# Retention step of an encoder layer: inner products of four chunks ahead of the cross products, and the turns of the norm factor at another place and in another kind of bank

## Chip, core and metric

The kernel runs on one core of one Trainium2 chip. The metric is the device time of one execution in microseconds. Before the change it is 1183.5 us, the median of three runs (1183.13 to 1184.19).

## What is computed

One layer of a bidirectional encoder on 1024 tokens of width 1024, in float32: an input projection, eight heads of retention and eight heads of windowed attention beside each other, an output projection with a layer norm, and a gated feed-forward block with a second layer norm. The change touches only the retention, of which the reference says, for one direction and chunks of 128 tokens:

```python
scores = jnp.einsum('bhncd,bhnsd->bhncs', q, k) * decay_in[None, :, None]
y_inner = jnp.einsum('bhncs,bhnse->bhnce', scores, v)
kv = jnp.einsum('bhnsd,bhnse->bhnde', k * k_decay[None, :, None, :, None], v)
...
_, r_prev = lax.scan(step, jnp.zeros((b, h, d, d), q.dtype), jnp.moveaxis(kv, 2, 0))
...
y_cross = jnp.einsum('bhncd,bhnde->bhnce', q * q_decay[None, :, None, :, None], r_prev)
return (y_inner + y_cross).reshape(b, h, s, d)
```

Both directions are added, each head is normed over its 64 values (the mean is taken out of the values beforehand, so only a mean square is left), multiplied with a gain, and gated.

## The kernel before

**Stages.** The first 120 us or so hold the first projections and the attention of the first pair of heads. Then four rounds of retention follow, one for each pair of retention heads (up to about 358 us in the profile); rounds 1, 2 and 3 carry the attention of their pair beside it. After that come the output projection, the first norm, and the feed-forward block.

**The order on TensorE is written out by hand.** `run(steps, total)` takes a list in which `F` stands for a share of the remaining projection work: a queue of triples of 512-column matmuls (lines 77, 78, 79; `F` takes some three or four triples at a time). So the list says after which piece of projection each piece of retention or attention stands. The other engines' order is not written out: a scheduler places their instructions, so an edit of the list also changes the order on VectorE and ScalarE.

**Names in the list.** With `hh` or `q` 0 or 1 for the first and second half of the tokens (four chunks of 128 each):

- `K(q)`: keys turned on TensorE (line 404) and scaled by their decay on VectorE. `r.kv`: the state updates (line 423). `r.scan`: the recurrence over chunks on VectorE, and four DMAs that put the states in place. `Q(q)`: scores (line 454), decayed on VectorE into `pt`, and queries with decay `qq` (line 459).
- `Y(hh)`, `Retention.out`: for each of four chunks the inner products (`pt` with the values `rv`, line 475) and the cross products (`qq` with `states`, line 477), all four chunks in one PSUM bank of the kind "o"; then a square of it on ScalarE (line 480) and a copy into `y` on VectorE (line 481).
- `M(hh)`, `Retention.norm`: sums of the squares by a small matmul (line 488), a power on GpSimd (line 491), and the factor spread out to `r` on ScalarE (line 493).
- `X(hh)`, `Retention.turn`: four turns (transposes) of `r` on TensorE (line 498) into a bank of the kind "t", and one multiply `y * gain * turned factor` on VectorE (line 500), which reads that bank.
- `sco(n)`, `trn(n)`, `val(n)`: for block n of the attention, scores (lines 527, 528, softmax on VectorE and ScalarE in lines 529 to 539), turns of the probabilities (line 551, one bank of kind "t" for each of two key groups, each copied out by ScalarE into `ptr`, line 553), and values (line 563, `ptr` with `av`, in a bank of kind "o").
- `presplit_*`: side work on VectorE, ScalarE and the SP queue's DMAs (lines 580 to 582) for later weights; `G` are the decays of the next round.

**Banks.** Each kind of bank ("mm", "s", "t", "o") has two, taken in turn. A new user of a kind waits until the readers of the one before last are done. `X(1)` and `M(1)` of a round stand in the next round's list (as `X1` and `M1`).

In rounds 1 to 3 the part of the list that matters is, before:

```python
run([*V, K(0), M1, F, K(1), sco(0), F, (r.kv,), Q(0), F, sco(1), X1, F, trn(0), sco(2), (r.scan,), F, trn(1),
...
     G[2], X(0), Y(1), val(4), val(5), F, trn(6), F, trn(7), F], 48)
```

Of the kernel before, what the change touches and what calls it, by code (L numbers as in the profile page):

```python
# [16 lines left out]
P = 128  # L17
# [25 lines left out]
def layer(tc, xT, xn, w_first, w_mt, w_rv, w_out, w_pg, w_pe, pT, w_gu, w_dn,  # L43
          consts, dec_b, dec_c, sink, gng, lnp, out):
    nc = tc.nc
    act, dve, pool, pe, sp = nc.scalar, nc.vector, nc.gpsimd, nc.tensor, nc.sync
# [12 lines left out]
    def nm(s):  # L59
        uid[0] += 1  # L60
        return f"{s}{uid[0]}"

    def bank(tag, shape=(P, HF)):
        tag = ROLE[tag]
        return ps.tile(list(shape), F32, tag=tag, bufs=NB[tag], name=nm("b" + tag))
# [67 lines left out]
    def bt(shape, tag, bufs=None, dt=F32):  # L133
        return bpool.tile(list(shape), dt, tag=tag, bufs=bufs, name=nm(tag))
# [15 lines left out]
    with tc.manual_schedule(engines={mybir.EngineType.DVE, mybir.EngineType.SP}):  # L150
        for kt in range(KT):
            r = xraw[kt]
# [107 lines left out]
    for h in range(2):  # L260
        sl = slice(h * HF, (h + 1) * HF)
        b = st[1, h]
        for g in range(2):
            a = slice(64 * g, 64 * g + 64)
# [14 lines left out]
    def take(k):  # L279
        for _ in range(min(k, len(queue))):  # L280
            queue.pop(0)()
            ticks[0] += 1
            for what in (later, side):
                for x in [x for x in what if x[0] <= ticks[0]]:
                    what.remove(x)
                    x[1]()

    def mtile(idx, evac):
        hold = {}

        def load():
            hold["w"] = unit2(w_mt[idx])

        def step(h, kt):
            if kt == 0:
                hold["b"] = bank("mm")
            b, w = hold["b"], hold["w"][kt // 4]
            c = slice((kt % 4) * P, (kt % 4 + 1) * P)
            sl = slice(h * HF, (h + 1) * HF)
            mm3(b, w[:, 0, c], w[:, 1, c], xs[kt][:, 0, sl], xs[kt][:, 1, sl], kt == 0, kt == KT - 1)  # L300
            if kt == KT - 1:
                evac(b, h)

        return [load], [lambda h=h, kt=kt: step(h, kt) for h in range(2) for kt in range(KT)]

    def enqueue(tiles):

        def both(f, g):
            f()
            g()  # L310

        for f in tiles[0][0]:
            f()
        for n, (_, steps) in enumerate(tiles):
            if n + 1 < len(tiles):
                for k, f in enumerate(tiles[n + 1][0]):
                    steps[2 * k] = lambda f=f, g=steps[2 * k]: both(f, g)
            queue.extend(steps)
# [16 lines left out]
    rv = bt([P, NT, HF], "rv")  # L335
# [52 lines left out]
    class Retention:  # L388
# [76 lines left out]
        def out(self, hh):  # L465

            o, pt, qq = bank("o", (P, 4, P)), self.pt[hh], self.qq[hh]
            for j in range(4):
                n = 4 * hh + j
                for part in range(2):  # L470
                    for h in range(2):
                        a = slice(64 * h, 64 * h + 64)
                        v = self.i * P + 64 * h
                        if part == 0:
                            pe.matmul(o[a, j, :], rv[:, n, v:v + 64], pt[:, h, j, :], start=True, stop=False)
                        else:
                            pe.matmul(o[a, j, :], self.states[:, h, n, :], qq[:, h, j, :], start=False, stop=True)
            of = o.rearrange("p n c -> p (n c)")
            sq = self.sq = bt([P, HF], "rb")
            act.activation(sq, of, AF.Square)  # L480
            dve.tensor_copy(self.half(hh), of)
            self.o = o

        def norm(self, hh):

# [7 lines left out]
            act.activation(r.rearrange("p n h e -> p (n h) e"), sm[:, 1, :].unsqueeze(2).to_broadcast([P, 8, 64]), AF.Copy)  # L493

        def turn(self, hh):
            tb = bank("t", (P, 4, P))
            for j in range(4):
                pe.transpose(tb[:, j, :], self.r[hh][:, j].rearrange("p h e -> p (h e)"), ident)
            y = self.half(hh)
            dve.scalar_tensor_tensor(y, y, gn[:, self.i:self.i + 1], tb.rearrange("p n c -> p (n c)"), ALU.mult, ALU.mult)  # L500
# [167 lines left out]
    def ytile(k):  # L668
        if ys[k] is None:
            ys[k] = a_tile([P, S], "y", "A0" if k < 4 else "A1")  # L670
        return ys[k]
# [24 lines left out]
    def gate(i):  # L696
        def f(b, h):
            s = bt([P, HF], "sq", 1)
            sl = slice(h * HF, (h + 1) * HF)
            act.activation(s, b, AF.Tanh, scale=0.5)  # L700
            dve.scalar_tensor_tensor(s, s, 1.0, b, ALU.add, ALU.mult)
            dve.scalar_tensor_tensor(ys[2 * i][:, sl], s, 0.5, ys[2 * i][:, sl], ALU.mult, ALU.mult)
        return mtile(10 + i, f)

    def run(steps, total):

        shares = steps.count(None)
        done = n = 0
        for f in steps:
            if f is None:  # L710
                n += 1
                take(total * n // shares - done)
                done = total * n // shares
            else:
                f[0](*f[1:])

    F = None
    with tc.manual_schedule(engines={mybir.EngineType.PE}):
        enqueue([mtile(0, ev_av), proj_rv(), *project(1), *project(2), *project(3), gate(0), gate(1), gate(2), gate(3)])

        spare.append(bt([P, S], "aq", 3, F32R))
        twin = lambda t: t.rearrange("p (a b) -> p a b", a=2)
        ops = [twin(spare[1]), a_tile([P, 2, HF], "pro", "A0", F32R)]
        side.extend(presplit_out(0, ops, 17.5, 4))
        side.extend(presplit_out(1, ops, 44, 4, spare[:1]))
        a = Attention(0, ytile(1))
        sco, trn, val = (lambda n: (a.scores, n)), (lambda n: (a.turn, n)), (lambda n: (a.values, n))
        run([F, F, sco(0), F, sco(1), F], 16)
        run([F, (av_turn, 0), (av_turn, 1), F, trn(0), sco(2), F, trn(1), sco(3), F, val(0), val(1), trn(2), sco(4), F,
             trn(3), sco(5), F, val(2), val(3), trn(4), sco(6), F, trn(5), sco(7), F, val(4), val(5), trn(6), (decay_q, 0),  # L730
             F, trn(7), (decay_k, 0, 0), F, val(6), val(7), (decay_k, 0, 1), F], 64)
        assert not side and not later
        y0 = ytile(0)
        side.extend(presplit_gate())
        states = state_tile()
        r = Retention(0, y0, states)
        K, M = (lambda q: (r.keys, q)), (lambda q: (r.norm, q))
        Q, X = (lambda q: (r.scores, q)), (lambda q: (r.turn, q))
        Y = lambda hh: (r.out, hh)
        run([K(0), F, K(1), F, F, (r.kv,), Q(0), F, (r.scan,), F, F, F, Y(0), Q(1),  # L740
             F, M(0), (decay_q, 1), F, (decay_k, 1, 0), X(0), Y(1), (decay_k, 1, 1), F, F], 48)
        V = []
        for i in range(1, NPAIR):
            assert i == 1 or not side, len(side)
            M1, X1 = M(1), X(1)
            r = Retention(i, ytile(2 * i), states)
            a = Attention(i, ytile(2 * i + 1))
            if i == 2:
                late = [ytile(6), ytile(7)]
                op = twin(late[1].bitcast(F32R))  # L750
                side.extend(presplit_out(2, [op], 2, 3.5, late[:1]))
                side.extend(presplit_small(0, op, 30) + presplit_small(1, op, 38))
            elif i == 3:
                op = twin(bt([P, S], "aq", 3, F32R))
                side.extend(presplit_out(3, [op], 4, 3.5, [bt([P, S], "rk", 2)]))
                side.extend(presplit_small(2, op, 32) + presplit_small(3, op, 40))
            G = [(f, i + 1, *x) for f, x in ((decay_q, ()), (decay_k, (0,)), (decay_k, (1,)))] if i + 1 < NPAIR else \
                [(lambda: None,)] * 3
            run([*V, K(0), M1, F, K(1), sco(0), F, (r.kv,), Q(0), F, sco(1), X1, F, trn(0), sco(2), (r.scan,), F, trn(1),
                 sco(3), F, val(0), val(1), F, trn(2), sco(4), F, trn(3), sco(5), F,  # L760
                 Y(0), val(2), val(3), Q(1), F, G[0], trn(4), sco(6), M(0), F, G[1], trn(5), sco(7), F,
                 G[2], X(0), Y(1), val(4), val(5), F, trn(6), F, trn(7), F], 48)
            V = [val(6), val(7)]
        run([*V, M(1), F, X(1), F, F], 16)

# [179 lines left out]
    X = four("a")  # L945
    product(1, X, True, a11)
    part = ct([P, 8, HF], "h0b")
# [21 lines left out]
    X = four("a")  # L969
# [121 lines left out]
    X = four("a")  # L1091
# [4 lines left out]
    pt = {t: load_p(t) for t in range(2)}  # L1096
# [20 lines left out]
    for k in range(4):  # L1117
        c = slice(k * P, (k + 1) * P)
# [15 lines left out]
    pt = {t: load_p(t) for t in range(2)}  # L1134
    Y = four("a")
    product(6, Y, True, TT[2], steps[6:8])
    es3.close()
# [160 lines left out]
    n = 0  # L1298
    for k, upto in enumerate((2, 4, 8, 12)):
        c = slice(k * P, (k + 1) * P)  # L1300
# [311 lines left out]
    with tc.manual_schedule(engines={ET.PE, ET.DVE, ET.Activation, ET.Pool, ET.SP}):  # L1612
        ahead(2, 4)
        for k in range(NG):
# [5 lines left out]
            j = k + 1 - NG  # L1620
# [103 lines left out]
```

## Time and profile before

| what | value |
| --- | --- |
| median of three runs | 1183.5 us |
| the profiled execution's own time | 1184.56 us |
| its span (first to last instruction) | 1182.8 us |
| TensorE matmul busy | 1169.2 us (99%) |
| VectorE, ScalarE, GpSimd busy | 765.8, 534.5, 366.1 us |
| matmul busy from 288 to 358 us (round 3) | 68.66 of 70.00 us |
| matmul busy from 358 to 420 us (output projection) | 61.73 of 62.00 us |
| clock granted to TensorE | 0.998 of full speed |

Lines such as L498 are line numbers of the kernel before. A timeline row has the start, the duration, the engine, the line, the operation, what it writes and reads, and in brackets how long the engine was idle before it and what ended that. PE is the matmul side of TensorE, PEld its weight load, DVE is VectorE, ACT ScalarE, POOL GpSimd. Matmuls are pipelined and their ends are modelled, so the spacing of their starts says more than their durations; in a steady run of projection triples the starts stand 0.23 us apart.

### The profile page before, as it was taken

How to read it: one execution, taken by the hardware profiler on the slowest of the kernel's cores; microseconds unless marked ns; L12 is line 12 of the kernel's file. 1: busy time of each engine (PE TensorE's matmuls, PEld its weight loads, DVE VectorE, ACT ScalarE, POOL GpSimd, SP SyncE). 2: the span in 40 equal slices, each digit the busy share in tenths (PEclk: the TensorE clock that was granted, in tenths of full speed). 3: DMA queues.
4: the chain of work that ended last, by engine and by line, in shares of the span. 5: the costliest groups of instructions: out<-in, count | busy, mean ns of one | idle time of the engine just before them, and what ended most of it. 6: DMA issues, size and time to landing. Idle time of an engine off the chain costs nothing.

```text
span 1182.8 us, 17057 instructions
## 1 busy us (share of the span) xinstructions
PE 1169.2 (99%) x6068; PEld 969.6 (82%) x6068; DVE 765.8 (65%) x1310; ACT 534.5 (45%) x1049; POOL 366.1 (31%) x346
## 2 busy tenths in 40 slices
PE   9999999999999999999999999999999999999997
PEld 7888888888888888888888888888888888888885
DVE  4666678775759688948655455545545465774677
ACT  5566347776756266214333333323333325562463
POOL 2001020202010021004755657464655341134232
PEclk9999999999999999999999999999999999999999
DMA  6345656546345945756223322233113179999977
GB/s 252 101 149 215 241 184 234 192 141 214 105 161 213 373 169 192 280 183 209 109 81 131 134 90 86 91 134 134 66 68 134 72 214 320 348 276 200 268 179 213
DMA packets 80661, 211.71 MB, mean 179 GB/s; under 512 B 9536, under 2 KB 14784, under 8 KB 80576
## 3 DMA queue, kind: packets, MB, share of 16 engines
q1 hardware_dynamic: 71936, 193.84, 46.4%
q0 software_dynamic: 8640, 16.78, 8.1%
q8 instruction: 48, 0.79, 0.3%
q14 instruction: 37, 0.30, 0.1%
HBM read 139.29 MB, written 62.13 MB: 170 GB/s over the span
## 4 chain that ended last, share of the span: by engine, by line
PE 87%; ACT 5%; DVE 4%; DMA 2%; issue 1%; POOL 0%; DVEq 0%; SPq 0%; ACTq 0%; POOLq 0%
PE bs L783 6%; PE bs L781 6%; PE bs L782 6%; PE bt L781 6%; PE bt L783 6%; PE bt L782 6%; PE bmm L783 5%; PE bmm L781 5%; PE bmm L782 5%; PE bo L782 5%; PE bo L783 5%; PE bo L781 5%; PE bmm L77 4%; PE bmm L78 4%; PE bmm L79 4%; ACT sc L533 1%
## 5 line engine op out<-in xcount | busy, mean ns | idle before, releaser
L77 PE MATMUL bmm<-H,w 128*128 128x512 f32 x240 | 97.6, 407 | 0.0
L78 PE MATMUL bmm<-H,w 128*128 128x512 f32 x240 | 94.2, 392 | 0.0
L79 PE MATMUL bmm<-H,w 128*128 128x512 f32 x240 | 94.1, 392 | 0.0
L1185 POOL TENSOR_TENSOR H<-ln 128x512 f32<-128x512 f32 x22 | 28.9, 1313 | 179.3 <-DMA ln<-in_w_gu 179.3
L1215 POOL TENSOR_TENSOR ev<-ev 128x512 f32<-128x512 f32 x33 | 55.0, 1667 | 90.2 <-DVE ev L1230 39.1
L72 DVE TENSOR_TENSOR w<-H,w 128x512 fp32r<-128x512 f32 x44 | 41.3, 939 | 62.5 <-ACT w L71 62.5
L72 DVE TENSOR_TENSOR w<-raw,w 128x512 fp32r<-128x512 f32 x56 | 46.0, 827 | 50.4 <-ACT w L71 50.2
L524 POOL COPY sc<-skb 128x1 f32<-128x1 f32 x64 | 14.7, 238 | 186.2 <-PE bt L551 166.8
L1213 ACT ACTIVATE ev<-ev 128x512 f32<-128x512 f32 x33 | 20.9, 632 | 102.7 <-DVE ev L1230 102.7
L1219 POOL TENSOR_TENSOR ev<-ev,ev 128x512 f32<-128x512 f32 x44 | 62.7, 1437 | 2.6
L72 DVE TENSOR_TENSOR u<-H,u 128x512 fp32r<-128x512 f32 x47 | 38.1, 810 | 36.9 <-ACT u L71 36.6
L77 PEld LDWEIGHTS bmm<-H,w 128*128 128x128 f32 x240 | 45.2, 188 | 10.6 <-issue 1.2
L79 PEld LDWEIGHTS bmm<-H,w 128*128 128x128 f32 x240 | 45.2, 188 | 10.1
L78 PEld LDWEIGHTS bmm<-H,w 128*128 128x128 f32 x240 | 45.3, 189 | 7.8
L71 ACT ACTIVATE u<-H 128x512 fp32r<-128x512 f32 x47 | 29.6, 630 | 44.1 <-POOL H L1186 8.3
L533 ACT ACTIVATE sc<-sc,st 128x385 f32<-128x385 f32 (+1 forms) x64 | 37.2, 584 | 18.3 <-DVE st L531 18.0
L71 ACT ACTIVATE w<-raw 128x512 fp32r<-128x512 f32 x56 | 34.5, 624 | 22.5 <-PE bo L79 8.8
L529 DVE CUSTOM_DVE_ANT_0 sc<-cst,bs,skb 128x384 f32<-128x384 f32 (+1 forms) x64 | 34.9, 575 | 8.7 <-PE bs L528 8.6
L491 POOL TENSOR_TENSOR sm<-sm,cst 128x8 f32<-128x8 f32 x8 | 14.3, 1791 | 79.1 <-DVE sm L490 79.1
L892 POOL TENSOR_TENSOR stt<-stt,cst 128x1 f32<-128x1 f32 x8 | 12.2, 1521 | 83.8 <-DVE stt L891 83.8
L1189 POOL TENSOR_TENSOR H<-raw,H 128x512 f32<-128x512 f32 x22 | 37.4, 1698 | 0.0
L71 ACT ACTIVATE w<-H 128x512 fp32r<-128x512 f32 x44 | 27.4, 622 | 21.8 <-PE bs L783 6.3
(810 smaller groups left out, 3765.0 us busy)
## 6 DMA issues: line engine op xcount, KB each, us to landing
ad<-ev SPq DMA_DIRECT2D x33, 512.0 KB, 2.6
pgd<-pro SPq DMA_DIRECT2D x28, 512.0 KB, 2.9
raw<-in_w_gu SPq DMA_DIRECT2D x22, 512.0 KB, 4.5
ln<-in_w_gu SPq DMA_DIRECT2D x22, 512.0 KB, 3.6
raw<-ad SPq DMA_DIRECT2D x40, 256.0 KB, 5.7
ln<-ad SPq DMA_DIRECT2D x37, 256.0 KB, 6.5
H<-in_w_dn SPq DMA_DIRECT2D x33, 256.0 KB, 7.6
wod<-aq SPq DMA_DIRECT2D x15, 512.0 KB, 2.7
```

Source lines behind the costliest of these rows:

```text
L71: act.activation(hi, raw, AF.Copy)
L72: dve.tensor_tensor(lo, raw, hi.bitcast(F32), ALU.subtract)
L77: pe.matmul(o, lh, rh, start=start, stop=False)
L78: pe.matmul(o, lh, rl, start=False, stop=False)
L79: recent[0] = pe.matmul(o, ll, rh, start=False, stop=stop).ins.name
L533: act.activation(sc[g][:, :nk + 1], sc[g][:, :nk + 1], AF.Exp, bias=st_[:, 1, j, g:g + 1], accum_out=st_[:, 2, j, g:g + 1])
L781: pe.matmul(o, lh, rh, start=start, stop=False, skip_group_check=True)
L782: pe.matmul(o, lh, rl, start=False, stop=False, skip_group_check=True)
L783: pe.matmul(o, ll, rh, start=False, stop=stop, skip_group_check=True)
L1189: pool.tensor_tensor(s[3], a(0, 1), s[0], ALU.subtract)
L1215: pool.tensor_tensor(c[:, 1, :], c[:, 0, :], c[:, 1, :], ALU.mult)
L1219: pool.tensor_tensor(self.ev[dst][:, 0, :], left, right, op)
```

## The change

Three edits. In `out`, all inner products of the four chunks are issued ahead of all cross products (before, they alternated chunk by chunk); only the first inner product of a bank marks the start of an accumulation. The square and the copy of the outputs become a step of their own, `E(hh)`. In the lists, `X(0)` no longer stands ahead of `Y(1)` but behind it (in round 0) or behind `Y(1)`, `val(4)` and `val(5)` (in rounds 1 to 3), with `E(1)` behind `X(0)`. And `turn` takes a bank of kind "t" for the first half but of kind "o" for the second half, `X(1)`.

```diff
         def out(self, hh):
             o, pt, qq = bank("o", (P, 4, P)), self.pt[hh], self.qq[hh]
-            for j in range(4):
-                n = 4 * hh + j
-                for part in range(2):
+            for part in range(2):
+                for j in range(4):
+                    n = 4 * hh + j
                     for h in range(2):
                         a = slice(64 * h, 64 * h + 64)
                         v = self.i * P + 64 * h
-                        if part == 0:
-                            pe.matmul(o[a, j, :], rv[:, n, v:v + 64], pt[:, h, j, :], start=True, stop=False)
-                        else:
-                            pe.matmul(o[a, j, :], self.states[:, h, n, :], qq[:, h, j, :], start=False, stop=True)
-            of = o.rearrange("p n c -> p (n c)")
+                        lhs, rhs = (rv[:, n, v:v + 64], pt[:, h, j, :]) if part == 0 else \
+                            (self.states[:, h, n, :], qq[:, h, j, :])
+                        pe.matmul(o[a, j, :], lhs, rhs, start=part == 0 and j == 0, stop=part == 1,
+                                  skip_group_check=True)
+            self.o = o
+
+        def evict(self, hh):
+            of = self.o.rearrange("p n c -> p (n c)")
             sq = self.sq = bt([P, HF], "rb")
             act.activation(sq, of, AF.Square)
             dve.tensor_copy(self.half(hh), of)
-            self.o = o
...
         def turn(self, hh):
-            tb = bank("t", (P, 4, P))
+            tb = bank("to"[hh], (P, 4, P))
...
         run([K(0), F, K(1), F, F, (r.kv,), Q(0), F, (r.scan,), F, F, F, Y(0), Q(1),
-             F, M(0), (decay_q, 1), F, (decay_k, 1, 0), X(0), Y(1), (decay_k, 1, 1), F, F], 48)
+        run([K(0), F, K(1), F, F, (r.kv,), Q(0), F, (r.scan,), F, F, F, Y(0), E(0), Q(1),
+             F, M(0), (decay_q, 1), F, (decay_k, 1, 0), Y(1), X(0), E(1), (decay_k, 1, 1), F, F], 48)
...
-                 Y(0), val(2), val(3), Q(1), F, G[0], trn(4), sco(6), M(0), F, G[1], trn(5), sco(7), F,
-                 G[2], X(0), Y(1), val(4), val(5), F, trn(6), F, trn(7), F], 48)
+                 Y(0), E(0), val(2), val(3), Q(1), F, G[0], trn(4), sco(6), M(0), F, G[1], trn(5), sco(7), F,
+                 G[2], Y(1), val(4), val(5), X(0), E(1), F, trn(6), F, trn(7), F], 48)
```

How the instructions stand on the engines: line numbers of the rows of the change are those of the changed file, two or three higher than before (498 becomes 500, 500 becomes 502, 481 becomes 484, 551 becomes 553, 563 becomes 565, 581 becomes 583; 475 and 477 become 476). The numbers behind the names tell buffers apart.

TensorE in round 2, from the last projection matmul ahead of `X(0)` on, before:

```order
L79 MATMUL bmm_2838<-H_232,w_2582 128x512
L498 MATMUL bt_2911<-cst,rb_2828 128x128 x4
L475 MATMUL bo_2917<-pt_2752,rv_444 64x128 x2
L477 MATMUL bo_2917<-qq_2765,states_1168 64x128 x2
...
L563 MATMUL bo_2937<-ptr_2798,av_442 64x128
L563 MATMUL bo_2937<-ptr_2804,av_442 64x128
```

and now:

```order
L79 MATMUL bmm_2838<-H_232,w_2582 128x512
L476 MATMUL bo_2911<-pt_2752,rv_444 64x128 x8
L476 MATMUL bo_2911<-qq_2765,states_1168 64x128 x8
L565 MATMUL bo_2928<-ptr_2798,av_442 64x128
L565 MATMUL bo_2928<-ptr_2804,av_442 64x128
...
L500 MATMUL bt_2941<-cst,rb_2828 128x128 x4
L77 MATMUL bmm_2838<-H_299,w_2582 128x512
```

The four turns stood between the projection and the outputs; now the outputs and the values come first, and the turns are the last thing ahead of the next projection matmul. Rounds 1 and 3 read the same.

TensorE in round 3, the turns `X1` and `trn(0)`, with the engines each row waits for; before:

```order
L498 MATMUL bt_3190<-cst,rb_3049 128x128 [waits Activation_49]
...
L551 MATMUL bt_3208<-cst,sc_3078 128x128 [waits Activation_49]
L551 MATMUL bt_3208<-cst,sc_3078 128x128
L551 MATMUL bt_3213<-cst,sc_3079 128x128 [waits DVE_49]
L551 MATMUL bt_3213<-cst,sc_3079 128x128
```

and now:

```order
L500 MATMUL bo_3190<-cst,rb_3049 128x128 [waits Activation_49]
...
L553 MATMUL bt_3208<-cst,sc_3078 128x128 [waits Activation_49]
L553 MATMUL bt_3208<-cst,sc_3078 128x128
L553 MATMUL bt_3213<-cst,sc_3079 128x128 [waits Activation_49]
L553 MATMUL bt_3213<-cst,sc_3079 128x128
```

The second key group of `trn(0)` waited for VectorE, that is for the multiply that reads the bank of `X1`; it now waits for ScalarE alone.

VectorE in round 1 around the multiply of `X(0)`, before:

```order
L531 TENSOR_SCALAR st_1912<-st_1912 128x2 [waits DVE_49]
L500 TENSOR_SCALAR y_1580<-y_1580,gn,bt_2180 128x512 [waits PE_49]
L537 RECIPROCAL st_1912<-st_1912 128x2 [waits Activation_49]
L581 TENSOR_TENSOR pro_1163<-pre_1159,pro_1163 128x512 [waits DMAHW1_49,Activation_49]
L481 COPY y_1580<-bo_2186 128x512 [waits Activation_49]
```

and now:

```order
L533 TENSOR_SCALAR st_1912<-st_1912 128x2 [waits DVE_49]
L539 RECIPROCAL st_1912<-st_1912 128x2 [waits Activation_49]
L583 TENSOR_TENSOR pro_1163<-pre_1159,pro_1163 128x512 [waits DMAHW1_49,Activation_49]
L502 TENSOR_SCALAR y_1580<-y_1580,gn,bt_2210 128x512 [waits PE_49]
L484 COPY y_1580<-bo_2180 128x512 [waits Activation_49]
```

The multiply (L500, now L502) has moved behind a subtraction of the side work that waits for ScalarE and a DMA. In round 3 it has moved behind such a subtraction too; in round 2 only behind the reciprocal. The order on GpSimd and on the SP queue is the same as before.

More of the change, by code (lines that the diff above doesn't have):

```diff
@@ L738, in layer @@
         Q, X = (lambda q: (r.scores, q)), (lambda q: (r.turn, q))
-        Y = lambda hh: (r.out, hh)
-        run([K(0), F, K(1), F, F, (r.kv,), Q(0), F, (r.scan,), F, F, F, Y(0), Q(1),
-             F, M(0), (decay_q, 1), F, (decay_k, 1, 0), X(0), Y(1), (decay_k, 1, 1), F, F], 48)
+        Y, E = (lambda q: (r.out, q)), (lambda q: (r.evict, q))
+        run([K(0), F, K(1), F, F, (r.kv,), Q(0), F, (r.scan,), F, F, F, Y(0), E(0), Q(1),
+             F, M(0), (decay_q, 1), F, (decay_k, 1, 0), Y(1), X(0), E(1), (decay_k, 1, 1), F, F], 48)
         V = []
```

## Prediction, made before the changed kernel ran

> **What bounds the kernel now.** I read the busy line of the page first, then the list of TensorE's waits, then the timeline around each wait in the retention rounds.
>
> ```profile
> PE 1169.2 (99%) x6068; PEld 969.6 (82%) x6068; DVE 765.8 (65%) x1310; ACT 534.5 (45%) x1049; POOL 366.1 (31%) x346
> PE bt L498 <- ACT ptr L553: 1.8, 3, 1.3
> PE bo L142 <- POOL sq L139: 1.3, 1, 1.3
> PE bt L551 <- DVE y L500: 1.2, 1, 1.2
> PE bt L781 <- ACT h0b L950: 0.3, 1, 0.3
> ```
>
> TensorE sets the time: busy for 99% of the span. The four other rows are its whole list of waits (total, times, longest). Two of them are the change's to take: the turns (L498) wait for ScalarE's copies of the attention's turns (L553), and the attention's turns (L551) wait for VectorE's multiply (L500). Neither outputs (L475, L477) nor values (L563) are in the list. So the room is a few microseconds of 1183.5. Because matmul ends are modelled, I measure these waits from starts. Here is `X(0)` in rounds 0 to 3, each with the projection matmul ahead of it:
>
> ```profile
> 155.69 0.39 PE L79 MATMUL bmm<-H,w 128*128 128x512 f32 x1
> 156.18 0.66 PE L498 MATMUL bt<-cst,rb 128*128 128x128 f32 x4
> 212.54 0.39 PE L79 MATMUL bmm<-H,w 128*128 128x512 f32 x1
> 213.27 0.66 PE L498 MATMUL bt<-cst,rb 128*128 128x128 f32 x4 [0.35 <-ACT ptr L553]
> 273.69 0.39 PE L79 MATMUL bmm<-H,w 128*128 128x512 f32 x1
> 275.38 0.66 PE L498 MATMUL bt<-cst,rb 128*128 128x128 f32 x4 [1.31 <-ACT ptr L553]
> 337.13 0.39 PE L79 MATMUL bmm<-H,w 128*128 128x512 f32 x1
> 337.67 0.66 PE L498 MATMUL bt<-cst,rb 128*128 128x128 f32 x4 [0.15 <-ACT ptr L553]
> ```
>
> The steps are 0.49, 0.73, 1.69 and 0.54 us, where a step without a wait takes 0.23: lost are 0.26, 0.50, 1.46 and 0.31, together 2.53 us.
>
> **Part 1, inner products ahead of cross products: 0.** It could only help where the cross products wait for `qq` or the states, and no row of the wait list names them. The count of matmuls is the same, and both kinds have one shape. The cover is long: in round 3 the states, the last operand of `Y(0)` to be made, are sent by DMAs that are issued 15 us or more ahead of its start (322.67, in a fence below):
>
> ```profile
> 305.20 2.39 SPq L443 DMA_DIRECT2D states<-kv  x4
> ```
>
> Without that cover the new order would hide up to the inner half of a `Y`, 0.9 us, of such a wait; no row gives it a loss.
>
> **Part 2, `X(0)` behind the outputs and values: -2.53 us.** `X(0)` waits for a bank that ScalarE empties (rounds 1 to 3) or for its factor `r` (round 0). Now `Y(1)`, whose operands are long there, fills that time. What is late next is `val(5)`, which needs both copies of `trn(5)`:
>
> ```profile
> 274.86 0.85 ACT L553 ACTIVATE ptr<-bt 128x384 f32<-128x384 f32 x2
> 275.97 0.44 PE L475 MATMUL bo<-pt,rv 128*64 128x128 f32 x4
> 277.77 1.48 PE L563 MATMUL bo<-ptr,av 128*64 128x128 f32 x24
> 338.54 0.47 ACT L553 ACTIVATE ptr<-bt 128x384 f32<-128x384 f32 x1
> ```
>
> `Y(1)` takes 277.77 - 275.97 = 1.80 us and `val(4)` about half of the values' 1.41, so `val(5)` starts about 0.33 + 1.80 + 0.7 = 2.8 us after the last projection matmul starts. The second copy ends 275.71 - 273.69 = 2.0 us after it in round 2 and 339.01 - 337.13 = 1.9 in round 3: 0.8 us to spare. I take 0; the other bound is the longest wait of this kind, 1.46.
>
> **Part 3, what the new neighbours cost: -0.40 us.** Going between the projection's shape (128*128) and the outputs' (128*64) spreads the starts. The rows that price it:
>
> ```profile
> 279.18 0.50 PE L77 MATMUL bmm<-H,w 128*128 128x512 f32 x1
> 279.51 0.40 PE L78 MATMUL bmm<-H,w 128*128 128x512 f32 x1
> 322.34 0.40 PE L79 MATMUL bmm<-H,w 128*128 128x512 f32 x1
> 322.67 0.44 PE L475 MATMUL bo<-pt,rv 128*64 128x128 f32 x4
> 226.52 0.66 PE L404 MATMUL bt<-cst,rk 128*128 128x128 f32 x4
> 227.01 0.73 PE L488 MATMUL bo<-cst,rb 128*128 128x2 f32 x6
> 238.83 0.60 PE L498 MATMUL bt<-cst,rb 128*128 128x128 f32 x4
> 239.19 0.48 PE L77 MATMUL bmm<-H,w 128*128 128x512 f32 x1
> 239.50 0.40 PE L78 MATMUL bmm<-H,w 128*128 128x512 f32 x1
> ```
>
> Before, without the wait: 0.23 to the turns, 275.97 - 275.38 = 0.59 from the turns to the outputs, 279.18 - 275.97 = 3.21 for outputs and values, 0.33 to the second projection matmul: 4.36. Now: 0.33 to the outputs (322.67 - 322.34), the same 3.21, the turns behind values (four turns after a change of shape 0.49, as for keys; the last one gives way to the projection after 0.03 where 0.11 would be a turn's pace: 0.41), and 239.50 - 239.19 = 0.31: 4.26. So 0.10 less, four times. The Trainium skill, "TensorEngine Tiling (Array Packing)", section Key Properties, says that a change of tiling mode drains TensorE; counted by that rule both orders change mode twice and this part is 0, the sum 0.40 smaller. The rows decide for -0.40, since what follows a change differs too. Bounds: -0.40 and 0.
>
> **Part 4, `X(1)` in a bank of kind "o": -1.39 us kept in round 3, nothing kept in round 1.** Before, the second key group of `trn(0)` waited for the bank of `X1`:
>
> ```profile
> 303.44 0.38 PE L551 MATMUL bt<-cst,sc 128*128 128x128 f32 x2
> 304.21 0.73 DVE L500 SCALAR_TENSOR_TENSOR y<-y,gn,bt 128x512 f32<-128x512 f32 x1
> 305.19 0.42 PE L527 MATMUL bs<-k,aq 128*128 128x384 f32 x1
> PEld bt L551 <- DVE y L500: 1.7, 2, 1.4
> 297.73 0.37 ACT L429 ACTIVATE kv<-bt 128x256 f32<-128x256 f32 x1
> ```
>
> Four turns take 0.36 us without a wait (238.83 to 239.19 above); here 1.75 (305.19 - 303.44), so 1.39 are lost. The weight loads' list of waits has this wait twice, 1.7 in all and 1.4 the longest: the other one, in round 1, is 0.3. `trn(0)` now gets the banks of `r.kv`, whose last copy in round 3 ends at 298.1, five microseconds ahead. Next in line is `trn(1)`, in rounds 1 and 3:
>
> ```profile
> 183.44 0.63 ACT L553 ACTIVATE ptr<-bt 128x256 f32<-128x256 f32 x2
> 183.86 0.20 PEld L551 LDWEIGHTS bt<-cst,sc 128*128 128x128 f32 x2 [0.26 <-ACT ptr L553]
> 306.07 1.12 ACT L539 ACTIVATE sc<-sc,st 128x384 f32<-128x384 f32 x2
> 308.74 0.82 PE L551 MATMUL bt<-cst,sc 128*128 128x128 f32 x6
> ```
>
> In round 1 it already starts the moment ScalarE frees its bank, and ScalarE is paced by VectorE: the 0.3 comes back whole (bounds 0 and 0.3). In round 3 it would start at 308.74 - 1.39 = 307.35, and its operand ends at 307.19; on VectorE the reciprocal ahead of it has moved behind two softmax passes, about 0.1 us later, so I charge 0.10 (the other bound is the whole 1.39).
>
> **Part 5, `E(1)` and the multiply: 0.** The square and copy of `Y(1)` are read by `M(1)`, which stands in the next round's list behind `val(6)`, `val(7)` and `K(0)`. `X(0)`'s multiply now frees a bank that `trn(6)` wants; in rounds 1 and 3 it is queued on VectorE behind a subtraction that waits for ScalarE and a DMA, and behind the multiply stand the copy and the projections' evictions (rival B prices a delay there). Nothing moved on SP or GpSimd, and no DMA moves.
>
> **Sum.** -2.53 - 0.40 - 1.39 - 0.3 + 0.3 + 0.10 = -4.22 us. The profiled execution (span 1182.8, own time 1184.56) would become 1180.3. It lies 1.06 above the median of the runs, so a median of 1183.5 becomes **1179.3**. The two ends: all kept, -4.6; either the largest price in part 2 or that in part 4 paid, about -2.8. That is 1178.9 to 1180.7.
>
> **Rivals.**
>
> A, *the wait moves with TensorE's lead.* Everywhere ScalarE and VectorE are paced by DMAs and each other, an earlier TensorE only waits at the next copy, as in round 1. If `val(5)` waits for all that `X(0)` no longer waits for, parts 3 and 4 are left: -0.40 - 1.39 + 0.10, about 1181.8. For it: the 0.26 at 183.86, where TensorE has no lead left. Against it: 0.8 us of slack at `val(5)`.
>
> B, *slower: the turns' bank.* `trn(6)` starts 2.18 us after the projection resumes, its second key group 0.3 later, and that takes the bank of `X(0)`, which the multiply must have read:
>
> ```profile
> 276.08 0.75 DVE L500 SCALAR_TENSOR_TENSOR y<-y,gn,bt 128x512 f32<-128x512 f32 x1 [0.98 <-PE bt L498]
> 281.36 0.81 PE L551 MATMUL bt<-cst,sc 128*128 128x128 f32 x6
> 300.91 0.60 PE L498 MATMUL bt<-cst,rb 128*128 128x128 f32 x4
> ```
>
> The multiply takes 0.75, so TensorE waits once it starts over 1.7 us behind the turns. The longest delay in these rounds is that of the multiply at 304.21, 2.9 us after `X1` was done (300.91 + 0.36). That would cost 1.2 us in each of rounds 1 to 3 and still leave a gain; it decides from a delay of 3.9 us (2.2 us a round, against 4.2 gained and 2.4 for a visible loss). Stuck behind a DMA for 4.5 us, as its place behind the subtraction allows, it costs 8.4: 1187.7. Against it: at 276.08 VectorE had been idle for 0.98 us and waited for the turns, which come later still now.
>
> C, *the gain is absorbed later,* where the output projection streams its weights: 1183.5. Against it: no wait for a DMA is in TensorE's list.
>
> **Numbers.** Forecast 0.71, A 0.13, B 0.11, C 0.05. A difference under 0.2% (2.4 us) counts as no change. The forecast's whole range is faster by more; A and C are within; B is slower: 0.71, 0.18, 0.11. The range takes the forecast's and most of A, and a little below for terms missed: 1178.2 to 1182.7.
>
> **What would show it.** Right: `X(0)` starts 0.20 us after the last value matmul without a wait; the second group of `trn(0)` follows the first at once in round 3; `trn(1)` of round 1 waits 0.3 us more; starts in the output projection are 4 us earlier. Wrong: waits of `val(5)` for L553, of `trn(6)` for the multiply, or new ones in round 3, where the orders of ScalarE and VectorE changed most.

## The result, and the profile after

| | before | after |
|---|---|---|
| median of the runs timed side by side, us | 1183.81 (1183.08 to 1184.9, 8 runs) | 1180.18 (1179.38 to 1180.73, 8 runs) |
| profiled execution: own time / span, us | 1184.56 / 1182.8 | 1180.62 / 1178.8 |
| predicted median, us | | 1179.3 (1178.2 to 1182.7) |

The ratio is 0.9969 with a 95% interval of 0.9958 to 0.998: faster by 3.6 us, 0.3%. Two more timings of the same program, described below, gave 0.9959 and 0.9958 (both 0.9946 to 0.9971). The prediction's ratio was 1179.3 / 1183.5 = 0.9965.

First the busy line of the changed kernel's page and TensorE's whole list of waits (engine, what it works on, what released it: total us, times, longest us). L500, L553, L555 and L783 are the lines that were L498, L551, L553 and L781.

```profile
PE 1167.3 (99%) x6068; PEld 968.4 (82%) x6068; DVE 767.3 (65%) x1310; ACT 534.4 (45%) x1049; POOL 365.5 (31%) x346
PE bo L142 <- POOL sq L139: 1.3, 1, 1.3
PE bs L783 <- DVE ev L1232: 0.7, 1, 0.7
PE bt L783 <- ACT h0b L952: 0.3, 1, 0.3
PE bmm L77 <- ACT H L71: 0.2, 1, 0.2
```

The waits of the turns for ScalarE's copies (1.8) and of the attention's turns for the multiply (1.2) are gone. One of 0.7 at L783, in the feed-forward stage, is new; it is followed up below. Next `X(0)` in rounds 0 to 3, with the projection matmul behind it, from TensorE's timeline (start, us, engine, line, operation):

```profile
157.21 0.66 PE L500 MATMUL bt<-cst,rb 128*128 128x128 f32 x4
157.62 0.48 PE L77 MATMUL bmm<-H,w 128*128 128x512 f32 x1
214.76 0.28 PE L565 MATMUL bo<-ptr,av 128*64 128x128 f32 x2
214.97 0.66 PE L500 MATMUL bt<-cst,rb 128*128 128x128 f32 x4
215.39 0.47 PE L77 MATMUL bmm<-H,w 128*128 128x512 f32 x1
275.55 0.66 PE L500 MATMUL bt<-cst,rb 128*128 128x128 f32 x4
275.96 0.47 PE L77 MATMUL bmm<-H,w 128*128 128x512 f32 x1
336.08 0.66 PE L500 MATMUL bt<-cst,rb 128*128 128x128 f32 x4
336.50 0.47 PE L77 MATMUL bmm<-H,w 128*128 128x512 f32 x1
```

The turns start 0.21 us behind the last pair of value matmuls (214.97 - 214.76), and the projection 0.41 us behind the turns, as the prediction put it. The same projection matmuls started, before, at these times (the one at 279.18 is in the prediction), and one near the program's start, of before and then of after, gives a zero:

```profile
8.68 0.39 PE L77 MATMUL bmm<-H,w 128*128 128x512 f32 x1
158.66 0.50 PE L77 MATMUL bmm<-H,w 128*128 128x512 f32 x1
217.07 0.50 PE L77 MATMUL bmm<-H,w 128*128 128x512 f32 x1
341.47 0.50 PE L77 MATMUL bmm<-H,w 128*128 128x512 f32 x1
```

```profile
7.97 0.39 PE L77 MATMUL bmm<-H,w 128*128 128x512 f32 x1
```

Lead means here how much earlier the same matmul, by its place in TensorE's order, starts than in the kernel before. So the changed kernel led by 0.7 us at 8.7 us already (another start-up, nothing of the change), by 1.04 after round 0, 1.68 after round 1, 3.22 after round 2, and 341.47 - 336.50 = 4.97 after round 3. In the retention rounds it gained 4.97 - 0.70 = 4.27 us; the prediction's sum was 4.22. The only place there where TensorE still loses more than a tenth of a microsecond is the attention's turns of chunk 1 in round 1:

```profile
182.25 0.39 PE L79 MATMUL bmm<-H,w 128*128 128x512 f32 x1
182.77 0.88 PE L553 MATMUL bt<-cst,sc 128*128 128x128 f32 x6
300.22 0.60 PE L553 MATMUL bt<-cst,sc 128*128 128x128 f32 x4
```

The step is 0.52 where 0.23 is free: the 0.3 that was to come back. In round 3 all four turns of chunk 0 now go in one group (300.22), without the 1.39 between its halves.

From there on about a microsecond goes again. The lead at the last matmul is 3.95 us. Between the matmuls that began at 534 and 575 us before, it falls from 4.97 to 3.65, and 0.3 comes back much later. The rows of the changed kernel, a weight load first, then TensorE's matmuls, then VectorE:

```profile
551.66 0.19 PEld L785 LDWEIGHTS bs<-H,w 128*128 128x128 f32 x1 [0.47 <-DVE w L72]
570.17 0.39 PE L785 MATMUL bs<-h,w 128*128 128x512 f32 x1
571.28 0.47 PE L783 MATMUL bs<-h,u 128*128 128x512 f32 x1 [0.72 <-DVE ev L1232]
570.46 0.67 DVE L1232 TENSOR_TENSOR ev<-ev,bs 128x512 f32<-128x512 f32 x1
```

At 551.66 a weight load waits for one of VectorE's subtractions, and about 0.36 us of the lead goes there. At 571.28 TensorE starts 1.11 us after the matmul ahead of it, where 0.23 is free, because VectorE's eviction of that bank ended at 571.1; with the next step that is 0.96. Before, no matmul there waits.

### The profile page after: what moved, and what is told of

The parts are those of the page before. It is cut to its first block, busy times and chain, and to the rows that moved or that the text cites. A ratio compares the mean times of both kernels' runs of the same rounds, so it can differ in the third digit from the quotient of the medians.

```text
span 1178.8 us, 17058 instructions
## 1 busy us (share of the span) xinstructions
PE 1167.3 (99%) x6068; PEld 968.4 (82%) x6068; DVE 767.3 (65%) x1310; ACT 534.4 (45%) x1049; POOL 365.5 (31%) x346
## 4 chain that ended last, share of the span: by engine, by line
PE 94%; DVE 3%; ACT 1%; issue 1%; DMA 1%; DVEq 0%; SPq 0%; ACTq 0%
PE bmm L77 6%; PE bs L785 6%; PE bs L783 6%; PE bs L784 6%; PE bmm L79 6%; PE bmm L78 6%; PE bt L783 5%; PE bt L785 5%; PE bt L784 5%; PE bmm L785 5%; PE bmm L783 5%; PE bmm L784 5%; PE bo L785 5%; PE bo L783 5%; PE bo L784 5%; PE bo L565 2%
```

## The experiments

Nine more kernels ran. One of them is the change once more, and another (evictions first) turned out to be the same program. For each the table has two lengths, worked out from the starts of the same matmul in its profiled execution and in that of the kernel before: what TensorE gained between the matmuls at 8.68 and 341.47 us (the retention rounds), and what it gave back between 341.47 and 575.24. Each length is from one execution. The third wait of the last two kernels lies just behind 341.47 and so in the second column. The ratio is to the kernel before, timed side by side.

| kernel | retention, us | given back, us | ratio, 95% interval |
|---|---|---|---|
| the change | -4.27 | +1.32 | 0.9969, 0.9958 to 0.998 |
| the change again | -4.28 | +0.21 | 0.9959, 0.9946 to 0.9971 |
| inner products first, alone | +0.13 | +1.09 | 1.0007, 0.9998 to 1.0016 |
| second half's bank, alone | -0.60 | +0.17 | 0.9996, 0.9987 to 1.0005 |
| the move, alone | -2.94 | +1.08 | 0.9970, 0.996 to 0.998 |
| both halves' bank, no move | -3.80 | +0.33 | 0.9965, 0.9951 to 0.9978 |
| turns of chunk 1 behind scores | -2.91 | +1.06 | 0.9973, 0.9963 to 0.9982 |
| evictions first (the change's program) | -3.72 | +0.08 | 0.9958, 0.9946 to 0.9971 |
| four copies ahead of the multiply | -2.61 | +1.51 | 0.9986, 0.9977 to 0.9996 |
| two copies ahead of the multiply | -2.33 | +2.30 | 0.9987, 0.9977 to 0.9996 |

**Inner products first, alone.** The kernel before with

```diff
-            for j in range(4):
-                n = 4 * hh + j
-                for part in range(2):
+            for part in range(2):
+                for j in range(4):
+                    n = 4 * hh + j
...
```

(and the accumulation marked as in the change).

> The kernel before with the inner products of four chunks ahead of all cross products and nothing else. My theory (part 1 of the prediction): 0, since no wait of TensorE before stands at a cross product; within 0.1% of the kernel before (1182.6 to 1185.0 us), and outputs that take the same time from first to last matmul (1.8 us). Rival: the order itself spreads or closes up the starts of the matmuls (other lhs per step, other part of the bank); with 8 outputs in all, 0.1 us each would be 0.8 us, to either side.

It made no difference: 1184.72 us beside 1184.67, and +0.13 us in the retention rounds. The order on VectorE, ScalarE and GpSimd is that of the kernel before, and yet the three waits of `X(0)` in rounds 1 to 3 are 0.22, 2.08 and 0.11 us where they were 0.50, 1.46 and 0.31. So a single one of these waits moves by up to 0.6 us though nothing that it waits for was changed; their sum (2.41 and 2.27) hardly does. The execution led by 1.05 us at the start and by 0.14 at its last matmul; 0.6 of that went at 534 us, at a wait for a DMA.

**The second half's bank, alone.** The kernel before with

```diff
-            tb = bank("t", (P, 4, P))
+            tb = bank("to"[hh], (P, 4, P))
```

> The kernel before with the turns of the second half in a bank of the outputs' kind, nothing moved. Theory (part 4): the 1.39 us wait at the attention's turns of chunk 0 in round 3 goes, the one of 0.3 in round 1 comes back at the turns of chunk 1: -1.3 us up to the end of the retention rounds, of which some may be given back in the feed-forward stage. X(0) still waits for ScalarE as before (0.50, 1.46, 0.31 in rounds 1 to 3). Rival: the bank also shifts ScalarE and VectorE in the round, the wait comes back at the attention's turns of chunk 1 in round 3 and the run equals the kernel before (0).

The wait in round 3 went, 1.40 us by the lead there, but only 0.60 was left at the end of the rounds. `X(0)` of rounds 2 and 3 in this kernel, each with the matmul ahead of it:

```profile
273.42 0.39 PE L79 MATMUL bmm<-H,w 128*128 128x512 f32 x1
275.51 0.66 PE L498 MATMUL bt<-cst,rb 128*128 128x128 f32 x4 [1.71 <-ACT ptr L553]
335.90 0.39 PE L79 MATMUL bmm<-H,w 128*128 128x512 f32 x1
336.76 0.66 PE L498 MATMUL bt<-cst,rb 128*128 128x128 f32 x4 [0.47 <-ACT ptr L553]
```

Lost are 2.09 - 0.23 = 1.86 and 0.86 - 0.23 = 0.63, where the kernel before lost 1.46 and 0.31. So neither expectation held: the gain was there and was not given back at chunk 1 of round 3. At the next `X(0)`, that of round 3, 0.32 of it went, since the copy that it waits for came only 0.91 us earlier (337.67 - 336.76) where TensorE was 1.23 earlier (337.13 - 335.90). The other 0.5 us were lost at `X(0)` of rounds 1 (0.10) and 2 (0.40), ahead of that gain and with ScalarE and VectorE still in the old order; the inner products alone lost 0.62 more at the same place of round 2. So that part can't be put down to the bank.

**The move, alone.** The changed kernel with the old order of products and the old bank:

```diff
-            tb = bank("to"[hh], (P, 4, P))
+            tb = bank("t", (P, 4, P))
...
```

> The changed kernel with the old order of the outputs' products and the old bank for the second half's turns: the move of X(0) behind outputs and values, and the eviction of its own, alone. Theory (parts 2 and 3): -2.53 -0.40 = -2.9 us up to the end of the retention rounds; the 1.4 us wait at the attention's turns of chunk 0 in round 3 stays. Rival A (the wait moves with TensorE's lead): the 1.46 us of round 2 comes back as a longer wait in round 3 and the run gains under 1.5 us.

-2.94 us where -2.9 was expected, and the wait in round 3 stayed as it was:

```profile
300.89 0.38 PE L553 MATMUL bt<-cst,sc 128*128 128x128 f32 x2
302.46 0.44 PE L553 MATMUL bt<-cst,sc 128*128 128x128 f32 x2 [1.19 <-DVE y L502]
```

Rival A falls in this form: the 1.46 of round 2 did not come back in round 3. The two parts alone give -0.60 - 2.94 = -3.54, together -4.27. The difference, 0.73, is about what the kernel with the bank alone lost more at the waits of `X(0)` (0.82), which the move takes away; how much of that would be there again in another execution is not shown.

**Both halves' turns in the outputs' kind of bank, nothing moved.** The kernel before with

```diff
-            tb = bank("t", (P, 4, P))
+            tb = bank("o", (P, 4, P))
```

> The kernel before with the turns of BOTH halves in banks of the outputs' kind and X(0) at its old place ahead of Y(1). Theory: the waits of X(0) for ScalarE's copies are waits for a bank, so they go without any move (0.50, 1.46, 0.31), and so does the 1.39 in round 3; the 0.26 of round 0 (a wait for the factor) stays, and the 0.40 of new neighbours is not had: about -3.6 us at the end of the retention rounds, some 0.7 us less than the change. Rival: the outputs' bank is not free at that place either (VectorE's multiply of X(0) and the copies of the outputs come late), Y(1) or M(1) waits for it, and less than half of that is left (-1.8 or less).

`X(0)` at its old place, in round 2, and ScalarE's copies of chunk 5, for which it used to wait:

```profile
272.17 0.39 PE L79 MATMUL bmm<-H,w 128*128 128x512 f32 x1
272.40 0.60 PE L498 MATMUL bo<-cst,rb 128*128 128x128 f32 x4
273.36 0.85 ACT L553 ACTIVATE ptr<-bt 128x384 f32<-128x384 f32 x2
```

It starts 0.23 us behind the projection, 0.96 us before the copies even begin. -3.80 us stand against -3.6 expected, and the ratio, 0.9965, can't be told from that of the change. So it is the bank that counts in rounds 1 to 3, and one changed letter takes most of what the whole change takes. The 0.48 us between this kernel and the change are the wait for the factor in round 0, which stays here (0.48 - 0.23 = 0.25 from the starts of these two rows), and 0.2 for the neighbours:

```profile
154.74 0.39 PE L79 MATMUL bmm<-H,w 128*128 128x512 f32 x1
155.22 0.66 PE L498 MATMUL bo<-cst,rb 128*128 128x128 f32 x4
```

**The change again.** No edit.

> The changed kernel once more, unaltered. In its first profiled execution TensorE was 4.27 us further ahead at the end of the retention rounds (counted from 8.7 us on), and 1.0 us of it was lost between 534 and 575 us, where VectorE runs behind. The bank-only and both-banks runs lost nothing there, the place-only run lost 1.0 too. Theory: that loss is chance of the single execution (which engine gets in first, VectorE or GpSimd), so this profile may have it or not, while the retention rounds repeat: -4.2 to -4.3. Rival: the loss belongs to this kernel's timing; then it is there again with about 1 us. Time 0.9955 to 0.998 of the kernel before either way.

The retention rounds repeat to 0.01 us, and only 0.2 us were given back. A third execution of the same program (evictions first, below) gained 3.72 and gave back 0.08, so the 0.01 is luck, and the loss in the feed-forward stage belongs to the execution. The rows behind it, of the first profile: the issue of a transfer of weights, ScalarE's first use of it, and VectorE's:

```profile
558.48 0.38 SPq L1179 DMA_DIRECT2D raw<-in_w_gu  x1
564.37 0.63 ACT L71 ACTIVATE u<-raw 128x512 fp32r<-128x512 f32 x1 [4.01 <-DMA raw<-in_w_gu]
565.03 1.18 DVE L72 TENSOR_TENSOR u<-raw,u 128x512 fp32r<-128x512 f32 x1 [3.41 <-ACT u L71]
```

And of the second:

```profile
558.28 0.38 SPq L1179 DMA_DIRECT2D raw<-in_w_gu  x1
562.85 0.63 ACT L71 ACTIVATE u<-raw 128x512 fp32r<-128x512 f32 x1 [2.96 <-DMA raw<-in_w_gu]
563.52 1.31 DVE L72 TENSOR_TENSOR u<-raw,u 128x512 fp32r<-128x512 f32 x1 [2.09 <-ACT u L71]
568.95 0.68 DVE L1232 TENSOR_TENSOR ev<-ev,bs 128x512 f32<-128x512 f32 x1
```

From issue to use it is 5.89 us in the one, 4.57 in the other. VectorE's evictions stand behind that step in its queue, and from the start of VectorE's step to that of the eviction for which TensorE waits it is the same time in both: 570.46 - 565.03 and 568.95 - 563.52 are 5.43 us. So a late transfer makes that eviction late by as much. The same rows of the other profiles part them in the same way. Issue to use is 5.79 to 6.01 us for the move alone, the turns behind scores and the two copies, and there the matmul starts 1.0 to 1.7 us behind the one ahead of it; it is 4.47 to 4.75 in the six others, the kernel before among them, and there the step is at most 0.28. Why the transfer takes longer in some executions was not found.

**Turns of chunk 1 behind the scores, in round 1.** The changed kernel, trying for the last 0.29 us:

```diff
-            run([*V, K(0), M1, F, K(1), sco(0), F, (r.kv,), Q(0), F, sco(1), X1, F, trn(0), sco(2), (r.scan,), F, trn(1),
-                 sco(3), F, val(0), val(1), F, trn(2), sco(4), F, trn(3), sco(5), F,
+            run([*V, K(0), M1, F, K(1), sco(0), F, (r.kv,), Q(0), F, sco(1), X1, F, trn(0), sco(2), (r.scan,), F, *((sco(3), trn(1)) if i == 1 else (trn(1), sco(3))),
+                 F, val(0), val(1), F, trn(2), sco(4), F, trn(3), sco(5), F,
```

> The changed kernel, and in round 1 the score products of chunk 3 stand ahead of the attention's turns of chunk 1, so that these come some 0.8 us later and no longer wait 0.29 us for ScalarE's copy. Theory: -0.3 us against the changed kernel in round 1, nothing elsewhere, unless the values of chunk 1 now wait for their turns' copies. Rival: ScalarE and VectorE are the pace there, the copies of chunk 1 come later by as much, and TensorE waits at the values instead: 0 or +0.3.

The rival held, and more strongly than it was put. The turns came 0.3 us later without a wait, but the second copy of chunk 1 on ScalarE then stood behind two more softmax passes and came at 187.54, where the changed kernel has it at 186.47, and the values waited:

```profile
187.54 0.48 ACT L555 ACTIVATE ptr<-bt 128x384 f32<-128x384 f32 x1
188.07 0.87 PE L565 MATMUL bo<-ptr,av 128*64 128x128 f32 x10 [1.32 <-ACT ptr L555]
```

It ends 1.4 us behind the change in the retention rounds.

**Evictions first.** The changed kernel with `E(1)` directly behind `Y(1)`:

```diff
-                 G[2], Y(1), val(4), val(5), X(0), E(1), F, trn(6), F, trn(7), F], 48)
+                 G[2], Y(1), E(1), val(4), val(5), X(0), F, trn(6), F, trn(7), F], 48)
...
```

(and so in round 0).

> The changed kernel with the square and copy of the second half's outputs put directly behind the outputs, ahead of the values and the turns of r, on ScalarE's and VectorE's lists too. Theory (part 5): 0, within 0.1% of the changed kernel, since M(1) that reads them comes a round later. Rival: the copy now stands ahead of the multiply on VectorE and of the copies of the attention's turns on ScalarE, and the values of chunk 5 or the attention's turns of chunk 6 wait: up to 0.7 us (one VectorE operation) a round, 2 us in all.

0.9958 beside 0.9959 for the change: no difference in the time, and none was possible. The profile has the same instructions in the same order on every engine and on the SP queue as that of the change, with the square and the copy still behind the multiply: the scheduler places `E(1)` by itself, wherever it stands in the list. So neither the theory nor the rival was tested. What the run gives is a third execution of the change, and a measure of how far executions differ: 0.55 us less gained in the retention rounds, of which 0.41 went at the attention's turns of chunk 7 in round 1 (they waited for a copy on ScalarE, which was over half a microsecond later than in the first profile) and 0.14 at score products in round 2.

**Four copies ahead of the multiply.** The changed kernel with, in `turn`,

```diff
+            if hh == 0 and self.i:
+                for _ in range(4):
+                    dve.tensor_copy(self.pt[1][:, 0], tb)
             dve.scalar_tensor_tensor(y, y, gn[:, self.i:self.i + 1], tb.rearrange("p n c -> p (n c)"), ALU.mult, ALU.mult)
```

> The changed kernel, and ahead of the multiply that reads X(0)'s bank VectorE makes four more copies of that bank (each 0.6 us of pace, written over a tile that is dead then) in rounds 1 to 3: the multiply starts 2.4 us later. Rival B's price as the prediction had it: the second key group of the attention's turns of chunk 6 takes that bank, 1.7 us of slack before a wait. In the changed kernel's profile the multiply of round 2 runs 276.25 to 277.0 and that group starts about 278.4, so 1.4 us of slack: TensorE should wait 0.7 to 1.0 us in each of the three rounds, +2 to +3 us against the changed kernel. If the bank is not the one that is taken next, there is no wait at the turns and the time stays within 0.5 us; then B never was a risk. Other waits further on, of work queued behind the multiply on VectorE, would be a third possibility.

The size fitted, +0.77 us in each round, and the reading behind it did not. Round 1: the second half of the six turns of chunk 6, ScalarE's copy of their first half, and the multiply.

```profile
217.81 0.49 ACT L558 ACTIVATE ptr<-bt 128x384 f32<-128x384 f32 x1 [0.43 <-PE bt L556]
218.36 0.55 PE L556 MATMUL bt<-cst,sc 128*128 128x128 f32 x3 [0.58 <-ACT ptr L558]
219.88 0.74 DVE L505 SCALAR_TENSOR_TENSOR y<-y,gn,bt 128x512 f32<-128x512 f32 x1
```

TensorE went on at 218.36, 1.5 us ahead of the multiply. With the multiply planned that late, the pool gave the second group the bank of the first, and the wait is for its copy. So the two banks of a kind are not always taken in turn, as was said of the kernel before. Here the delay that the planner saw cost no more than that at the turns. It did cost something further on, where TensorE had waited for no transfer; the rows of its list of waits:

```profile
PE bt L786 <- DMA u<-wod: 0.4, 1, 0.4
PE bt L786 <- DMA w<-wod: 0.3, 1, 0.3
```

These are weights of the output projection (at 362.42 and 363.71 us), and 0.7 us of the 1.51 went there: rival C's mechanism. That the added copies made these transfers late is likely, but not shown.

**Two copies.** The same edit with `range(2)`, where the second group still takes `X(0)`'s bank.

> The run with four copies showed a wait of 0.78 us in each of three rounds, but TensorE did not wait for the multiply there: with the multiply planned that late, the second key group of the attention's turns of chunk 6 was given the first group's bank and waited for ScalarE's copy of it. Here VectorE makes two copies of X(0)'s bank ahead of the multiply (written over a tile that is dead then); with one operation that is planned between them, the multiply comes three operations of 0.6 us, 1.8 us, later, and the second group still takes X(0)'s bank. In the changed kernel the multiply ends 1.45 us ahead of that group's start (277.0 and 278.45 in round 2). Rival B's mechanism: TensorE waits for the multiply, 0.35 to 0.45 us in each of rounds 1 to 3, about +1.1 us, and the group starts right behind the multiply's end. If the group starts on time although the multiply is still running, the bank was not what B said and a delay there is free: 0.

Rounds 1 and 2, VectorE's multiply and the second group:

```profile
217.33 0.74 DVE L505 SCALAR_TENSOR_TENSOR y<-y,gn,bt 128x512 f32<-128x512 f32 x1
218.21 0.52 PE L556 MATMUL bt<-cst,sc 128*128 128x128 f32 x3 [0.35 <-DVE y L505]
279.12 0.73 DVE L505 SCALAR_TENSOR_TENSOR y<-y,gn,bt 128x512 f32<-128x512 f32 x1
280.00 0.52 PE L556 MATMUL bt<-cst,sc 128*128 128x128 f32 x3 [1.04 <-DVE y L505]
```

Now the group starts 0.14 and 0.15 us behind the multiply's end. It loses 0.5 us in rounds 1 and 3, and 1.2 in round 2, where the operation between the copies itself waited for ScalarE: 2.2 us in all, against 1.1 expected. The multiply came 0.7 us later behind the projection there than in round 1 (2.82 and 2.12 us), and TensorE lost 0.7 more: lateness that nobody planned, in one operation on VectorE, went to TensorE whole. Rival B's mechanism is real; in the three executions of the change it is not reached.

No version was clearly faster than the change. What is left to take in its retention rounds is the 0.29 us in round 1, less than these timings can tell.

## Why the prediction was right

By its own steps, with the lead of TensorE in the two profiles of the change:

| step | predicted, us | measured, us |
|---|---|---|
| `X(0)` and its neighbours, round 0 | -0.26 - 0.10 | -0.34, -0.35 |
| `X(1)`'s bank, round 1: gained, given back | -0.3, +0.3 | -0.32 and +0.27, twice |
| `X(0)`, round 1 | -0.50 - 0.10 | -0.59, -0.62 |
| `X(0)`, round 2 | -1.46 - 0.10 | -1.54, -1.50 |
| `X(1)`'s bank and chunk 1, round 3 | -1.39 + 0.10 | -1.39, -1.40 |
| `X(0)`, round 3 | -0.31 - 0.10 | -0.36, -0.36 |
| sum | -4.22 | -4.27, -4.28 |

**Part 1** was 0, and alone it was 0. **Part 2:** all four waits of `X(0)` went and `val(5)` did not wait. That those of rounds 1 to 3 are waits for a bank, not for the place, the kernel with both halves' banks shows; the one of round 0 stayed there. **Part 3** came out nearly to size. From the last projection matmul ahead of `X(0)` to the second one behind it, the span that the prediction summed, TensorE gains 0.36, 0.62, 1.57 and 0.42 us in both profiles of the table, together 2.97; 2.53 of it are the waits, so the neighbours give 0.44, or 0.11 a round where 0.10 was forecast. (The rows of the table end at the first projection matmul and also hold hundredths lost elsewhere.) The Trainium skill's rule, "TensorEngine Tiling (Array Packing)", section Key Properties, counted by changes of mode alone, would give 0 there; the measurement lies with the rows. **Part 4** held in both rounds; the 0.10 charged to chunk 1 of round 3 did not come. **Part 5** held for the multiply, which made nothing wait; whether `E(1)` stands ahead of `X(0)` or behind it in the list turned out to do nothing.

That the sum was met to 0.05 us is in part luck: the third execution of the same program gained 3.72 us, and the three timings give -3.6 and, by the ratio, -4.9 and -5.0 us.

**Rival A** holds where it was seen, in round 1, and for 0.32 us in the kernel with the bank alone, but not for the change, whose `X(0)` no longer waits. **Rival B** has the right mechanism with a slack a little too large: the prediction let the multiply start 1.7 us behind the turns, that is behind the start of the projection after them, and it costs TensorE from 1.6 (the two copies: 217.33 is 2.12 behind that start at 215.21, and 0.5 was lost). The 0.1 between are the 0.14 us that the group starts behind the multiply's end. **Rival C**, a loss in the output projection to weights that arrive late, was not seen there for the change; but the feed-forward stage, where the prediction had looked for nothing, gave back about a microsecond in one of its three executions, by weights that arrive late too. That is the missing term: most of what the first two profiles of the change differ by. Whether it also parts the timings can't be said, since their intervals overlap.

## What to carry to other kernels

- When TensorE waits for a copy that empties a bank, ask first whether another kind of bank is free at that moment: here one letter, with no move at all, took 3.80 us where the change took 3.72 to 4.28.
- A wait whose end is set by another engine can absorb part of what is gained ahead of it (`X(0)` of round 3 took 0.32 of 1.40 us), so gains upstream and the wait itself have to be taken together.
- A buffer that a pool hands out follows the planned order: to test the cost of a late reader, look whether the same buffer is still the one that is taken.
- Compare the order of the instructions before reading an experiment: one edit of the list here left the program as it was. And take more than one profile: three of one program differed by 0.55 us in the retention rounds.

## What the runs showed of the hardware

A 512 KB transfer of weights on the same queue at the same place took 4.5 to 4.75 us from issue to use in seven of the eleven profiles and 5.8 to 6.0 in four, and about a microsecond of the program hangs on it. The first projection matmuls also have two paces: in the profile of before they start 0.43 us apart up to 7 us, in that of after 0.23 from 5.5 us on, at the same granted clock (1.00); the cause was not looked for.

VectorE's subtractions take 0.68 us alone and up to 1.78 beside GpSimd's own, as in these rows of the changed kernel, three of VectorE and one of GpSimd:

```profile
551.53 1.78 DVE L72 TENSOR_TENSOR u<-H,u 128x512 fp32r<-128x512 f32 x1
553.23 1.78 DVE L72 TENSOR_TENSOR w<-H,w 128x512 fp32r<-128x512 f32 x1
554.94 0.68 DVE L72 TENSOR_TENSOR u<-H,u 128x512 fp32r<-128x512 f32 x1
552.73 1.74 POOL L1191 TENSOR_TENSOR H<-raw,H 128x512 f32<-128x512 f32 x1
```

Once the last of GpSimd's row of subtractions has ended at 554.5, VectorE is back at 0.68. The subtraction for which the weight load at 551.66 waited, 0.36 us of the lead, was one of the slow ones (1.77 us, from 549.84 on). The Trainium skill, "Trainium Architecture — The Big Picture", section What this means for kernel authors, says that the two engines share a pair of ports under an exclusive lock; these rows agree.
